# A decoder layer on one core: sums for the first block of each up projection by DMA and GpSimd, the residual turned later, the last norm by token tile

## The chip, the cores and the metric

The kernel runs on one core of one Trainium2 chip. The metric is the device time of one execution in microseconds (us). The core's engines are TensorE (PE, with its weight loads PEld), VectorE (DVE), ScalarE (ACT), GpSimd (POOL) and SyncE (SP), which issues most transfers here; each runs its own instructions in order and waits for the others by semaphores.

## The reference

One layer of a decoder: 512 tokens of 1024 features, 256 memory tokens, a feed-forward width of 2816, all fp32.

```python
def swiglu(x, w_gu, w_down):
    gate, up = jnp.split(x @ w_gu, 2, axis=-1)
    return (jax.nn.silu(gate) * up) @ w_down

def reference(x, mem, ...):
    h = x
    h = h + 0.5 * swiglu(rms_norm(h, g_ffn1), w_ffn1_gu, w_ffn1_down)
    h = h + hybrid_mixer(rms_norm(h, g_mix), ...)
    h = h + memory_cross_attention(rms_norm(h, g_cross), rms_norm(mem, g_mem), ...)
    h = h + 0.5 * swiglu(rms_norm(h, g_ffn2), w_ffn2_gu, w_ffn2_down)
    return rms_norm(h, g_final)
```

The change touches the two feed-forward parts (`swiglu`) and the last `rms_norm`.

## The kernel before

Each feed-forward part is an up projection (`up`), whose result is spilled to HBM, and a down projection (`down`). Both are computed as Strassen-Winograd products: a 2x2 split of tokens and weights takes seven products P1 to P7 instead of eight, of sums of quarters. Every fp32 operand is split in a high and a low part (`split_hi` on ScalarE, line 117; `split_lo` on VectorE, line 123), and `mm_strassen` (lines 425 to 431) makes three matmuls of each pair.

The up projection has six blocks of columns, five of 512 and a last of 256. `UP` gives the order of the products in a block: P1, P2, P5, P3, P6, P7, P4. A product has two token halves with 12 matmuls each. `BANK` says which PSUM banks they accumulate in: P3 goes on in the banks that P5 opened ("C"), P6, P7 and P4 in those of P1 ("A"). Between the two products of a bank, `evac` copies the first result out (`a_...` in the listings, line 487, by ScalarE), so P3's first matmul of a token half stands behind the copy of that half of P5.

The weights of a block come as two units (0 and 1) of 1024 columns. `Weights.load` (line 392) has SyncE load three tiles for each: `x1` (quarter b11), `x2` (b22) and `x3` (b21). `Weights.make` splits the tile that a product needs into `whi` and `wlo` and then turns it into the next sum. `EARLY`, the table for the ups, names for each product the tile to split and the tile that the sum takes: after P1 and P3 an accumulating transfer adds b12 from HBM (line 418, issued by GpSimd), after P5 VectorE adds x3 to x1 (line 420), after P6 it adds x1 to x2 (line 422). The pool has buffers for six `x1`, three `x2`, six `x3`.

The token side has four quarters a11, a21, a12, a22 in two tiles, made once per up (`prepare`). Four sums of 128x1024 (line 462, VectorE) turn them into the others: v = a22 - a21 and a21 = a11 - a21 at P5, a11 = v + a11 and a12 = a11 - a12 at P3. Each product's side is split once, in block 0, into two `s` tiles, and kept.

`Plan` emits the units four ahead of the product in turn (`UNITS_AHEAD`) and the loads five ahead of that (`LOADS_AHEAD`). A scheduler then sets the order on each engine, and a load waits until a buffer of its pool is free. In an up the products depend on the split of their weights, of their side, and on the bank.

In `down`, three sets of pairs (a, b, c: four, four and three pairs of chunks of the 2816) go through seven products in the order `DOWN` = P1, P5, P6, P3, P7, P2, P4; P1 and P5 are run as P1a, P1b, P5a, P5b, P1c, P5c. Units 4 and 5 of the weights are those of set c. The sides are read back from the spill (line 591). Each result is added to the residual in token order, `ht` (line 607). Ahead of the products stands `before`: in the first down a load of `ht`, in the second `turn_back` (line 1088), which makes `ht` by 32 transposes of `h` and eight copies on ScalarE (line 1096).

After each result's last addition `squares2` sums the squares of one half of a token tile (line 1101). At the end `both` adds the two halves' sums for all four token tiles, `ro.newton` (lines 287 to 305) makes the reciprocal roots in 12 operations on 128x4, and four operations of 128x1024 (line 1110) scale by root and gain. Four transfers of 512 KB write the output (line 1112).

## Time and profile before

| | |
|---|---|
| time, median of 3 runs | 1454.97 us (1453.27 to 1457.66) |
| profiled execution | 1453.23 us |
| its span, first to last instruction | 1451.5 us |
| mean granted TensorE clock | 0.976 |
| busy: TensorE, VectorE, ScalarE, GpSimd | 96%, 65%, 51%, 6% |
| the first up, block 0; a block without waits | 58.16 us; 39.88 us |
| the second up, block 0 | 54.83 us |
| last matmul to end | 12.97 us |

The page has the busy shares; the stretches are those of the program's blocks, from the first matmul of one to the first of the next. A matmul of 512 columns stands 0.23 us behind the one before at full clock. A wait is shown ahead of the instruction that waited, with the engine that ended it. Instructions are told by line and by their tiles with buffer numbers left out, so `x` is any weight tile and `s` any side.

### The profile page before, as it was taken

The page shows a single profiled execution, that of the slowest core. Times are in us where ns is not written, and L with a number is a line of the kernel's source. Part 1 is how long each engine was busy: PE and PEld are TensorE (multiplying, and loading weights), DVE is VectorE, ACT ScalarE, POOL GpSimd, SP SyncE. Part 2 cuts the span into 40 slices and gives each one's busy share as a digit, 9 for nine tenths or more (in the row PEclk, how much of TensorE's full clock was granted, in tenths as well). Part 3 has the DMA queues.
Part 4 walks back from the last instruction along what each step waited for, and adds up shares of the span by engine and source line. Part 5 has one row for each costly group of instructions (what it writes and reads, how often), then busy time and mean ns, then how long its engine had stood idle before and what let it go on. Part 6 is the DMA issues. An engine that isn't in the chain of part 4 may idle for free.

```text
span 1451.5 us, 16735 instructions
## 1 busy us (share of the span) xinstructions
PE 1387.9 (96%) x6548; PEld 1162.3 (80%) x6548; DVE 949.7 (65%) x1237; ACT 735.6 (51%) x947; POOL 83.3 (6%) x102
## 2 busy tenths in 40 slices
PE   8899999999899999999999999999987999987996
PEld 7688888778788888888888888988865888876885
DVE  4877777696656664676544447655448777865884
ACT  6555565464565554566332225444335555554562
POOL 0011111110000000000000000000000111101000
PEclk8999999999999999999999999999988999998998
DMA  8676666871522233222223224444165666667461
GB/s 305 145 192 183 183 181 192 270 168 54 178 83 87 65 139 106 69 87 87 88 89 114 87 90 143 145 149 142 58 203 161 181 174 166 157 203 228 123 174 58
DMA packets 48303, 207.17 MB, mean 143 GB/s; under 512 B 5152, under 2 KB 5152, under 8 KB 39392
## 3 DMA queue, kind: packets, MB, share of 16 engines
q1 hardware_dynamic: 32624, 149.22, 29.6%
q0 software_dynamic: 15600, 56.89, 17.7%
q8 instruction: 51, 0.84, 0.2%
q14 instruction: 28, 0.23, 0.0%
HBM read 183.80 MB, written 22.28 MB: 142 GB/s over the span
## 4 chain that ended last, share of the span: by engine, by line
PE 83%; issue 5%; DMA 4%; DVE 4%; ACT 3%; POOL 0%; DVEq 0%; ACTq 0%; POOLq 0%
PE ps L153 13%; PE ps L155 13%; PE ps L154 13%; PE ps L430 11%; PE ps L429 11%; PE ps L431 11%; DMA x<-in_w_gu 2%; DVE wlo L123 2%; PE ps L250 2%; PE ps L249 2%; PE ps L251 1%; PE z L809 1%; ACT whi L117 1%; DMA x<-in_w_dt 1%; PE ps L521 1%
## 5 line engine op out<-in xcount | busy, mean ns | idle before, releaser
L429 PE MATMUL ps<-whi,s 128*128 128x512 f32 (+1 forms) x980 | 379.6, 389 | 31.8 <-ACT whi L117 11.7
L430 PE MATMUL ps<-wlo,s 128*128 128x512 f32 (+1 forms) x980 | 377.1, 385 | 3.3 <-DVE wlo L123 3.2
L431 PE MATMUL ps<-whi,s 128*128 128x512 f32 (+1 forms) x980 | 376.1, 384 | 0.5 <-DVE s L123 0.5
L123 DVE TENSOR_TENSOR wlo<-x,whi 128x1024 fp32r<-128x1024 f32 (+1 forms) x238 | 281.2, 1189 | 113.5 <-ACT whi L117 112.5
L117 ACT ACTIVATE whi<-x 128x1024 fp32r<-128x1024 f32 (+1 forms) x238 | 243.8, 1031 | 214.9 <-PE ps L431 128.9
L153 PE MATMUL ps<-a,whi 128*128 128x512 f32 (+1 forms) x832 | 318.2, 383 | 3.8 <-ACT whi L117 3.8
L155 PE MATMUL ps<-a,wlo 128*128 128x512 f32 (+1 forms) x832 | 318.0, 382 | 0.0
L154 PE MATMUL ps<-a,whi 128*128 128x512 f32 (+1 forms) x832 | 317.7, 382 | 0.0
L117 ACT ACTIVATE whi<-raw 128x1024 fp32r<-128x1024 f32 x120 | 127.1, 1060 | 269.0 <-PE ps L154 177.6
L429 PEld LDWEIGHTS ps<-whi,s 128*128 128x128 f32 x980 | 188.9, 193 | 70.4 <-ACT whi L117 15.3
L430 PEld LDWEIGHTS ps<-wlo,s 128*128 128x128 f32 x980 | 188.8, 193 | 41.4 <-DVE wlo L123 7.2
L431 PEld LDWEIGHTS ps<-whi,s 128*128 128x128 f32 x980 | 188.9, 193 | 35.7 <-DVE s L123 1.0
L123 DVE TENSOR_TENSOR wlo<-raw,whi 128x1024 fp32r<-128x1024 f32 x120 | 146.5, 1222 | 84.4 <-ACT whi L117 84.2
L153 PEld LDWEIGHTS ps<-a,whi 128*128 128x128 f32 x832 | 157.1, 189 | 34.1 <-ACT whi L117 4.1
L155 PEld LDWEIGHTS ps<-a,wlo 128*128 128x128 f32 x832 | 156.9, 189 | 31.1 <-DVE wlo L123 0.8
L154 PEld LDWEIGHTS ps<-a,whi 128*128 128x128 f32 x832 | 157.0, 189 | 30.4 <-DVE a L125 0.2
L418 POOL DMA_DIRECT2D x<-in_w_gu x44 | 38.5, 874 | 1077.6 <-DVE wlo L123 1035.9
L117 ACT ACTIVATE a<-a 128x512 fp32r<-128x512 f32 (+2 forms) x61 | 34.0, 557 | 59.5 <-DVE a L113 19.3
L113 DVE TENSOR_TENSOR a<-ps,a 128x512 f32<-128x512 f32 (+1 forms) x56 | 36.1, 649 | 38.8 <-PE ps L155 38.5
L123 DVE TENSOR_TENSOR s<-s,s 128x1024 fp32r<-128x1024 f32 (+1 forms) x36 | 40.6, 1129 | 17.3 <-ACT s L117 16.3
L123 DVE TENSOR_TENSOR a<-a,a 128x512 fp32r<-128x512 f32 (+2 forms) x61 | 36.2, 600 | 15.5 <-ACT a L117 11.6
L487 ACT ACTIVATE a<-ps,ny 128x512 f32<-128x512 f32 (+1 forms) x48 | 31.0, 650 | 28.8 <-PE ps L431 27.0
(162 smaller groups left out, 1326.5 us busy)
## 6 DMA issues: line engine op xcount, KB each, us to landing
x<-in_w_gu SPq DMA_DIRECT2D x66, 512.0 KB, 6.3
x<-in_w_gu POOLq DMA_DIRECT2D x44, 512.0 KB, 5.7
spilled<-e POOLq DMA_DIRECT2D x22, 896.0 KB, 7.5
x<-in_w_dn SPq DMA_DIRECT2D x30, 512.0 KB, 5.1
s<-spilled SPq DMA_DIRECT2D x28, 512.0 KB, 4.5
x<-in_w_dn POOLq DMA_DIRECT2D x20, 512.0 KB, 7.7
raw<-in_w_qk SPq DMA_DIRECT2D x8, 1024.0 KB, 4.9
raw<-in_w_v SPq DMA_DIRECT2D x8, 1024.0 KB, 5.2
```

What stands on the lines that cost most here:

```text
L113: nc.vector.tensor_tensor(out=out_, in0=a, in1=b, op=ALU.mult)
L117: nc.scalar.activation(hi, src, AF.Copy)
L123: nc.vector.tensor_tensor(out=lo, in0=src, in1=hi.bitcast(F32), op=ALU.subtract)
L153: nc.tensor.matmul(ps, wh, xh, start=first, stop=False, **kw)
L154: nc.tensor.matmul(ps, wh, xl, start=False, stop=False, **kw)
L155: nc.tensor.matmul(ps, wl, xh, start=False, stop=last, **kw)
L249: nc.tensor.matmul(ps[t], xh[:, c], hi[:, k, :], start=kk == 0, stop=False)
L418: nc.gpsimd.dma_start(out=x, in_=self.src[u][1], accum_op=ALU.add)
L429: nc.tensor.matmul(ps, ah, bh, start=first and k == 0, stop=False, **kw)
L430: nc.tensor.matmul(ps, ah, bl, start=False, stop=False, **kw)
L431: nc.tensor.matmul(ps, al, bh, start=False, stop=last and k == len(parts) - 1, **kw)
L487: nc.scalar.activation(a[key], ps, func, scale=scale)
```

## The change

Five edits:

1. Block 0 of each up uses a third table, `DMA_ONLY`: `x1` gets all three of its sums by accumulating transfers (b12 after P1's split, b21 after P5's, b22 after P6's), and P4 splits `x1` instead of `x2`. The four additions on VectorE fall away there, and four transfers come. `x2` is free after P2's split, `x3` after P7's as before.
2. The token sums run on GpSimd, and all four are issued at P5.
3. In `down`, `before` is issued behind the first two products (P1a, P1b) instead of ahead of all.
4. The last norm runs for each token tile as soon as its two halves are final (`finish`): 13 small operations on one column, then for half 1 a product with the gain on VectorE and a scaling on ScalarE, for half 0 one operation on VectorE, and an output transfer of 256 KB for each half.
5. Units 4 and 5, which only a down has, get buffers of their own (`x1b`, `x3b`, two each), and `x1` and `x3` have four instead of six. So in an up four tiles of each can be loaded ahead, and the down's last units are loaded during the first blocks of the up.

```diff
--- before.py
+++ after.py
@@ -391,7 +391,8 @@
 
         def load(self, x, u):
             def fn():
-                t = pools["w"].tile([P, 1024], F32, tag=x, name=nm(x), bufs=xbufs[x])[:, :self.size[u]]
+                tag = x if u < 4 or x == "x2" else x + "b"
+                t = pools["w"].tile([P, 1024], F32, tag=tag, name=nm(x), bufs=xbufs[tag])[:, :self.size[u]]
                 nc.sync.dma_start(out=t, in_=self.src[u][self.STARTS[x]])
                 self.t[x, u] = t
 
@@ -399,27 +400,29 @@
 
 
 
-        EARLY = {1: ("x1", "x1"), 2: ("x2", "x2"), 5: ("x1", "x3"), 3: ("x3", "x3"), 6: ("x1", "x2"),
-                 7: ("x3", "x3"), 4: ("x2", "x2")}
-        LATE = {**EARLY, 2: ("x2", "x1"), 6: ("x1", "x1"), 4: ("x1", "x1")}
+
+        EARLY = {1: ("x1", 1), 2: ("x2", None), 5: ("x1", "x3", "x1"), 3: ("x3", 1), 6: ("x1", "x1", "x2"),
+                 7: ("x3", None), 4: ("x2", None)}
+        LATE = {**EARLY, 2: ("x2", "x2", "x1"), 6: ("x1", None), 4: ("x1", None)}
+        DMA_ONLY = {**EARLY, 5: ("x1", 2), 6: ("x1", 3), 4: ("x1", None)}
 
         def unit(self, i, u):
-            x, y = self.chain[i]
-            return self.plan.unit(lambda: self.make(i, u), max(self.at[x, u], self.at[y, u]))
+            tiles = [x for x in self.chain[i] if isinstance(x, str)]
+            return self.plan.unit(lambda: self.make(i, u), max(self.at[x, u] for x in tiles))
 
         def make(self, i, u):
-            x, y = (self.t[k, u] for k in self.chain[i])
+            x, *then = self.chain[i]
+            x = self.t[x, u]
             hi, lo = (pools["w"].tile([P, 1024], F32R, tag=tag, name=nm(tag), bufs=xbufs["w"])
                       for tag in ("whi", "wlo"))
             m = self.size[u]
             split_hi(hi[:, :m], x)
             split_lo(lo[:, :m], x, hi[:, :m])
-            if i in (1, 3):
-                nc.gpsimd.dma_start(out=x, in_=self.src[u][1], accum_op=ALU.add)
-            elif i == 5:
-                nc.vector.tensor_tensor(out=x, in0=x, in1=y, op=ALU.add)
-            elif x is not y and i in (6, 2):
-                nc.vector.tensor_tensor(out=y, in0=y, in1=x, op=ALU.add)
+            if len(then) == 2:
+                src, dst = (self.t[k, u] for k in then)
+                nc.vector.tensor_tensor(out=dst, in0=dst, in1=src, op=ALU.add)
+            elif then[0] is not None:
+                nc.gpsimd.dma_start(out=x, in_=self.src[u][then[0]], accum_op=ALU.add)
             return [(hi[:, j:j + self.n], lo[:, j:j + self.n]) for j in range(0, m, self.n)]
 
     def mm_strassen(ps, sides, units, first, last, **kw):
@@ -430,7 +433,7 @@
             nc.tensor.matmul(ps, ah, bl, start=False, stop=False, **kw)
             nc.tensor.matmul(ps, al, bh, start=False, stop=last and k == len(parts) - 1, **kw)
 
-    xbufs = dict(x1=6, x2=3, x3=6, w=5)
+    xbufs = dict(x1=4, x1b=2, x2=3, x3=4, x3b=2, w=5)
 
     def up(g, r, w_gu, begin, norm):
 
@@ -459,14 +462,13 @@
             a11, a21, a12, a22 = (box[k] for k in ("a11", "a21", "a12", "a22"))
 
             def sum_(out, a, b, op):
-                nc.vector.tensor_tensor(out=out, in0=a, in1=b, op=op)
+                nc.gpsimd.tensor_tensor(out=out, in0=a, in1=b, op=op)
 
 
             if i == 5:
                 box["v"] = half(pools["w"].tile([P, 1024], F32, tag="wlo", name=nm("v"), bufs=xbufs["w"]))
                 sum_(box["v"], a22, a21, ALU.subtract)
                 sum_(a21, a11, a21, ALU.subtract)
-            elif i == 3:
                 sum_(a11, box["v"], a11, ALU.add)
                 sum_(a12, a11, a12, ALU.subtract)
             src = {1: a11, 2: a12, 5: box.get("v"), 3: a12, 6: a11, 7: a21, 4: a22}[i]
@@ -533,7 +535,7 @@
             per = 1024 // n
             units = 4 // per
             w = Weights(plan, [[w_gu[row + q * units + u] for q in range(4)] for u in range(units)], n,
-                        Weights.EARLY)
+                        Weights.EARLY if b else Weights.DMA_ONLY)
             row += 4 * units
             for x in w.STARTS:
                 for u in range(units):
@@ -617,12 +619,13 @@
             if a + m == n:
                 evac(i, t, ps)
 
-        plan.step(before)
         cuts = list(range(0, n, 4))
 
         order = [(i, a) for i in DOWN[:2] for a in cuts[:-1]] + [(i, cuts[-1]) for i in DOWN[:2]]
         order += [(i, a) for i in DOWN[2:] for a in cuts]
-        for i, a in order:
+        for place, (i, a) in enumerate(order):
+            if place == 2:
+                plan.step(before)
             m = min(a + 4, n) - a
             sd = side(i, a, m)
             us = []
@@ -1084,7 +1087,6 @@
             gain = pools["h"].tile([P, D], F32, name="gain")
             nc.sync.dma_start(out=gain, in_=g_final.partition_broadcast(P))
             sums2 = spool.tile([P, 8], F32, name="sums2", bufs=1)
-            ro = Norm()
 
             def turn_back():
                 for t in range(4):
@@ -1096,20 +1098,33 @@
                         nc.scalar.activation(ht[:, t, half * 512:(half + 1) * 512], ps, AF.Copy)
 
             def squares2(i, t):
-                for tok, half in {2: ((t, 0),), 3: ((t, 1),), 7: ((t + 2, 1),), 4: ((t + 2, 0),)}.get(i, ()):
-                    sq = pools["a"].tile([P, 512], F32, tag="sq", name=nm("sq"))
-                    nc.scalar.activation(sq, ht[:, tok, half * 512:(half + 1) * 512], AF.Square,
-                                         accum_out=sums2[:, 4 * half + tok:4 * half + tok + 1])
+                tok, half = {2: (t, 0), 3: (t, 1), 7: (t + 2, 1), 4: (t + 2, 0)}.get(i, (None, None))
+                if tok is None:
+                    return
+                sq = pools["a"].tile([P, 512], F32, tag="sq", name=nm("sq"))
+                nc.scalar.activation(sq, ht[:, tok, half * 512:(half + 1) * 512], AF.Square,
+                                     accum_out=sums2[:, 4 * half + tok:4 * half + tok + 1])
+                if i in (2, 4):
+                    finish(tok)
+
+            def finish(tok):
+
+                ro = Norm(P)
+                both = spool.tile([P, 1], F32, tag="both", name=nm("both"))
+                nc.vector.tensor_tensor(out=both, in0=sums2[:, tok:tok + 1], in1=sums2[:, 4 + tok:5 + tok], op=ALU.add)
+                ro.newton(both)
+                for half in (1, 0):
+                    c = slice(half * 512, (half + 1) * 512)
+                    o = ht[:, tok, c]
+                    if half:
+                        mul(o, o, gain[:, c])
+                        nc.scalar.activation(o, o, AF.Copy, scale=ro.cols)
+                    else:
+                        nc.vector.scalar_tensor_tensor(out=o, in0=o, scalar=ro.cols, in1=gain[:, c], op0=ALU.mult,
+                                                       op1=ALU.mult)
+                    nc.sync.dma_start(out=out[tok][:, c], in_=o)
 
             down(spilled, ht, w_dn2, w_dt2, turn_back, squares2)
-            both = spool.tile([P, 4], F32, name="both", bufs=1)
-            nc.vector.tensor_tensor(out=both, in0=sums2[:, :4], in1=sums2[:, 4:], op=ALU.add)
-            ro.newton(both)
-            for t in range(4):
-                o = ht[:, t, :]
-                nc.vector.scalar_tensor_tensor(out=o, in0=o, scalar=ro.cols[:, t:t + 1], in1=gain, op0=ALU.mult,
-                                               op1=ALU.mult)
-                nc.sync.dma_start(out=out[t], in_=o)
 
 
 def _tiles(w):
```

Three places show how the instructions now stand. First GpSimd's queue at the start of the second up: `x_8282` and `x_8284` are the `x1` tiles of units 0 and 1, `x_8290` and `x_8292` the `x3` tiles, `x_8268` holds a11 and a21, `x_8269` a12 and a22; `x_8299` and later are of block 1. Before:

```order
L418 DMA x_8282<-in_w_gu 128x1024
L418 DMA x_8284<-in_w_gu 128x1024
L418 DMA x_8290<-in_w_gu 128x1024
L418 DMA x_8292<-in_w_gu 128x1024
L418 DMA x_8299<-in_w_gu 128x1024
L418 DMA x_8311<-in_w_gu 128x1024
```

Now:

```order
L425 DMA x_8282<-in_w_gu 128x1024
L425 DMA x_8284<-in_w_gu 128x1024
L465 TENSOR_TENSOR v_8323<-x_8269,x_8268 128x1024
L465 TENSOR_TENSOR x_8268<-x_8268 128x4x256
L465 TENSOR_TENSOR x_8268<-v_8323,x_8268 128x4x256
L425 DMA x_8282<-in_w_gu 128x1024
L465 TENSOR_TENSOR x_8269<-x_8268,x_8269 128x4x256
L425 DMA x_8284<-in_w_gu 128x1024
L425 DMA x_8290<-in_w_gu 128x1024
L425 DMA x_8292<-in_w_gu 128x1024
L425 DMA x_8282<-in_w_gu 128x1024
L425 DMA x_8284<-in_w_gu 128x1024
```

The four sums stand behind P1's two transfers, and the second transfer into each `x1` stands among or behind them; a third into each follows those of `x3`.

Second, ScalarE in the same block: `whi_8454` and `whi_8459` are the splits of P6's weights, `a_8437` and `a_8452` the copies of P5's two token halves, `s_8376`, now `s_8372`, is P3's side. Before:

```order
L117 ACTIVATE whi_8410<-x_8290 128x1024
L117 ACTIVATE whi_8415<-x_8292 128x1024
L117 ACTIVATE whi_8454<-x_8282 128x1024
L487 ACTIVATE a_8437<-ps_8424,negr_8267 128x512
L117 ACTIVATE s_8376<-x_8269 128x1024
L499 ACT_TABLE_LOAD
L499 ACTIVATE a_8343<-a_8343 128x512
L499 ACTIVATE a_8358<-a_8358 128x512
L119 ACTIVATE s_8420<-x_8268 128x1024
L487 ACTIVATE a_8452<-ps_8439,negr_8267 128x512
L117 ACTIVATE whi_8459<-x_8284 128x1024
```

Now:

```order
L117 ACTIVATE whi_8408<-x_8290 128x1024
L117 ACTIVATE s_8372<-x_8269 128x1024
L117 ACTIVATE whi_8415<-x_8292 128x1024
L501 ACT_TABLE_LOAD
L501 ACTIVATE a_8345<-a_8345 128x512
L119 ACTIVATE s_8420<-x_8268 128x1024
L501 ACTIVATE a_8360<-a_8360 128x512
L489 ACTIVATE a_8437<-ps_8424,negr_8267 128x512
L117 ACTIVATE whi_8454<-x_8282 128x1024
L117 ACTIVATE whi_8459<-x_8284 128x1024
L489 ACTIVATE a_8452<-ps_8439,negr_8267 128x512
```

Both splits for P6 stand between P5's two copies; P6's first stood ahead of the first copy and the second behind the last one before.

Third, ScalarE where the second down begins: `e` are the last columns' turned results, which are spilled then, `ht` the copies of the turned residual; `whi_10273` (now `whi_10225`) is the first split for P5a. Before:

```order
L117 ACTIVATE whi_10273<-x_10191 128x1024
L523 ACTIVATE e_10112<-ps_10113 128x512
L523 ACTIVATE e_10112<-ps_10119 128x512
L1096 ACTIVATE ht_10137<-ps_10141 128x512
L1096 ACTIVATE ht_10137<-ps_10147 128x512
```

Now:

```order
L117 ACTIVATE whi_10225<-x_10143 128x1024
L525 ACTIVATE e_10112<-ps_10113 128x512
L525 ACTIVATE e_10112<-ps_10119 128x512
L117 ACTIVATE whi_10232<-x_10145 128x1024
L117 ACTIVATE whi_10317<-x_10149 128x1024
L117 ACTIVATE whi_10324<-x_10151 128x1024
L117 ACTIVATE s_10239<-s_10177 128x1024
L1098 ACTIVATE ht_10137<-ps_10267 128x512
```

Three more splits of weights and one of a side now stand ahead of the first `ht` copy.

## Rows read from the trace of the kernel before

**Rows 1.** The page, its span and the busy time of each engine.

```profile
span 1451.5 us, 16735 instructions
...
PE 1387.9 (96%) x6548; PEld 1162.3 (80%) x6548; DVE 949.7 (65%) x1237; ACT 735.6 (51%) x947; POOL 83.3 (6%) x102
```

**Rows 2.** Stretch, us; busy PE, PEld, DVE, ACT, POOL; PEclk, DMA share, GB/s.

```profile
32.12:68.62 36.50, 30.98 (x121) 24.37 (x120) 30.71 (x33) 20.02 (x23) 3.44 (x4) 0.91 0.57 140
81.21:108.50 27.29, 27.29 (x123) 22.61 (x122) 19.03 (x23) 14.81 (x18) 4.21 (x5) 1.00 0.94 251
256.31:292.23 35.92, 31.49 (x140) 24.90 (x138) 22.78 (x25) 16.92 (x21) 3.87 (x5) 1.00 0.84 260
1088.64:1129.46 40.82, 32.94 (x121) 25.39 (x121) 32.79 (x33) 23.20 (x27) 3.44 (x4) 0.87 0.58 157
1091.65:1101.75 10.10, 8.98 (x24) 6.36 (x25) 10.10 (x10) 7.32 (x9) 0.00 (x0) 0.66 0.07 30
1318.47:1363.57 45.10, 37.12 (x174) 30.92 (x173) 25.73 (x28) 21.68 (x29) 3.38 (x4) 0.89 0.65 184
1438.53:1451.50 12.97, 0.00 (x0) 0.00 (x0) 7.69 (x18) 0.72 (x2) 0.00 (x0) 0.64 0.40 162
```

**Rows 3.** Timeline of TensorE, second up: start, us, instructions [idle before <- releaser].

```profile
1088.03 0.39 PE L430 MATMUL ps<-wlo,s 128*128 128x512 f32 x1
1088.26 0.39 PE L431 MATMUL ps<-whi,s 128*128 128x512 f32 x1
1091.65 0.50 PE L429 MATMUL ps<-whi,s 128*128 128x512 f32 x1 [3.01 <-ACT s L117]
...
1116.85 0.73 PE L429 MATMUL ps<-whi,s 128*128 128x512 f32 x2 [3.73 <-ACT whi L117]
```

**Rows 4.** Timeline of TensorE, block 0 of the first up.

```profile
39.84 0.73 PE L429 MATMUL ps<-whi,s 128*128 128x512 f32 x2 [2.11 <-ACT s L117]
...
43.25 0.80 PE L429 MATMUL ps<-whi,s 128*128 128x512 f32 x1 [2.21 <-ACT s L119]
```

**Rows 5.** Chain of waits, start of the second up: start, us, what.

```profile
1076.40 0.85 POOL x L418
...
1077.28 12.22 DMA x<-in_w_gu
```

**Rows 6.** DMA issues: how many, KB each, median us to landing.

```profile
x<-in_w_gu POOLq DMA_DIRECT2D x44, 512.0 KB, 5.7
...
out_t<-ht SPq DMA_DIRECT2D x4, 512.0 KB, 2.8
```

**Rows 7.** Timeline of SyncE, start of the second up.

```profile
1066.21 11.74 SPq L395 DMA_DIRECT2D x<-in_w_gu  x15
```

**Rows 8.** Line 462, the token sums: durations min/median/max, first and last start.

```profile
L462 DVE TENSOR_TENSOR v<-x,x x2: 1217/1217/1217, 26.5 to 1080.3; 128x1024 f32<-128x1024 f32 x2
```

**Rows 9.** Timeline of GpSimd, start of the first up.

```profile
12.17 1.99 POOL L418 DMA_DIRECT2D x<-in_w_gu  x2 [10.66 <-DVE wlo L123]
```

**Rows 10.** Groups of GpSimd's own work: busy, mean ns, idle before.

```profile
L707 POOL MEMSET fence<- 128x512 f32 x1 | 0.5, 526 | 52.1 <-ACT sq L682 52.1
L710 POOL TENSOR_SCALAR_AFFINE_SELECT fence<-fence 128x256 f32<-128x256 f32 x1 | 0.4, 393 | 0.0
...
L103 POOL MEMSET ones<- 128x128 f32 x1 | 0.2, 204 | 0.3 <-POOLq L1209 0.3
```

**Rows 11.** Timeline of TensorE, start of the second down.

```profile
1319.99 3.11 PE L1094 MATMUL ps<-ident,h 128*128 128x128 f32 x27
1331.08 0.80 PE L429 MATMUL ps<-whi,s 128*128 128x512 f32 x1 [7.98 <-ACT ht L1096]
```

**Rows 12.** Chain of waits, start of the second down.

```profile
1324.39 5.88 DMA spilled<-e
```

**Rows 13.** Timeline of VectorE, the tail.

```profile
1440.11 0.16 DVE L1106 TENSOR_TENSOR both<-sums 128x4 f32<-128x4 f32 x1 [0.85 <-ACT sq L1101]
...
1442.68 4.87 DVE L1110 SCALAR_TENSOR_TENSOR ht<-ht,ny,gain 128x1024 f32<-128x1024 f32 x4
```

## The prediction, made before the change was run

> **What bounds the kernel now.** I read the page first. TensorE is busy 96% of a span of 1451.5 us [rows 1], so only its idle time, its time at the lower clock and the tail can be won; the other engines matter through what TensorE waits for. The profiled execution took 1453.23 us, 1.74 under the median of the runs; the sums are made against it.
>
> Next the busy time by stretch [rows 2]. From P5 on, the last five products of an undisturbed block take 27.29 us. The same five take 36.50 in block 0 of the first up and 40.82 in the second, where TensorE is busy 30.98 and 32.94 at a granted clock of 0.91 and 0.87. So at most 9.2 and 13.5 us can be won there. In the second down, the time from the last up product to the start of P6 is 45.10, in the first 35.92. After the last matmul 12.97 us pass.
>
> Then TensorE's timeline in those stretches, for what ended each wait. Second up: P2's last matmul begins at 1088.26 and they stand 0.23 apart; P5 then waits 3.01 us for `s` on ScalarE and P7 3.73 for a `whi` [rows 3]. First up: P3 waits 2.11 and, for its second token half, 2.21, both for `s` [rows 4]. A wait costs more than itself: P5 of the second up, which follows one, takes 10.10 at clock 0.66 [rows 2] (between its two levels, 1.2 and 2.4 GHz, so about two thirds of it at half clock) against 5.44, 24 matmuls at 0.227. The chain of waits names the origin [rows 5]: the accumulating transfer of P5's second weight sum, issued 1077.28, lands 12.22 later, while the median of its kind is 5.7 [rows 6]; 15 loads were issued from 1066.21 on, most of them ahead of it [rows 7].
>
> **Weight sums and buffers.** Per up, four VectorE additions of 128x1024 (1.22 us each, as the token sums of that shape [rows 8]) go and four accumulating transfers come, issued in 0.87 us each on POOL (two in 0.85 and more at 1076.40, two in 1.99 at 12.17 [rows 5, 9]). VectorE is rid of 4.9 us, which TensorE does not see by itself. What counts is when the sums land. With four x1 and x3 buffers 9 loads are free at the start of an up instead of 15; the tenth waits for the split of P2's first tile. So the first sums, for P5, meet a shorter burst. I take a landing 5.7 to 9 us after issue: in the second up the last comes between 1083.0 and 1086.3, before P2 ends, and P5 starts near 1088.6 without its 3.01.
>
> The second sums, for P6, can leave only when P5's weights are split: about 1088 and 1089 to 1091 for the two units. They land 5.7 to 12.22 later; the later unit between 1094.7 and 1101.4, both taken with an early issue for the late landing. **This is the new wait.** On ScalarE the splits of these sums (`whi_8454`, `whi_8459`) now stand ahead of `a_8452`, the copy of P5's second token half, and P3 accumulates into the bank that this copy empties. Without a wait P3's second half would start at 1088.6 + 5.44 + 2.72 = 1096.8. The copy, about 1.7 us behind the landing, ends between 1096.4 and 1103.1: a stall of 0 to 6.3, and up to 4.7 more for slow matmuls behind it (10.10 less 5.44). From 13.5 that leaves 2.5 to 13.4; **I take 9**, as the sums leave when few loads are under way. In the first up the same order holds (`whi_364`, `whi_369`, `a_362`): the two waits of [rows 4] go, the second sums leave about 28 and land between 34 and 41, against 40.3 for P3's second half, with a side split and three copies behind them on ScalarE. Off the 9.2 goes a stall of 1.2 to 5.2, with up to 4.7 behind it: -0.7 to 8, **I take 4**.
>
> **Token sums on GpSimd.** Eight of 128x1024, four per up. No row shows an addition on POOL. Nearest are fills of 128x512 (526 ns) and 128x128 (204), so 0.84 ns a column and 0.1 us fixed, and a select of 128x256 in 393 [rows 10]: one pass over 1024 columns is 1.0 us, three (two operands and a result) 2.8; these are the ends. I take two passes, 1.9, since the select, which reads and writes, is over a fill's rate (0.32 by that). In the second up POOL has issued both first sums at 1077.28 + 0.87 = 1078.2; v ends at 1080.1, the third sum at 1083.9, and only the fourth stands behind an issue that waits for P5's split, done at about 1091. P3's side needs it at 1094.1. Even at 2.8 the first three end at 1086.6, before that split. Nothing is on the path: cost 0, with up to 1 of the range for ends at 2.8.
> The Trainium skill, page GPSIMD Engine Reference, section Performance versus the Vector engine, speaks against this move: it gives an fp32 addition of 2048 columns as 4497 ns on GpSimd and 2293 on VectorE. An estimate from that page is 2.25 us for 1024 columns; no run here shows it yet, and by it the sum would be the same.
>
> **Residual turned later.** 32 transposes of 128x128 (27 of them in 3.11 [rows 11], so 3.7 in all) and eight copies leave the place behind the last up product and now stand behind two products of the down, whose spilled tiles landed long ago. So P1's first two products run while the last spill lands (5.88 us from 1324.39 [rows 12]), where TensorE now waits 7.98 [rows 11]. The first down, where the residual comes by a transfer, is the model: 35.92 [rows 2], plus 3.7 is 39.6 against 45.10, a gain of 5.5. Of those 35.92, 4.43 are idle (31.49 busy at full clock), for weight sums of the down's last pieces; with the new buffers these pieces are loaded in block 0 or 1, so up to 9.9. **I take 9**, nearer the end without waits. If P5 must wait for copies and banks, the 3.7 count twice at most, 5.5 again.
>
> **Last norm per token tile.** Before, 13 small operations of about 0.2 run from 1440.11, then four scaled products in 4.87 from 1442.68 [rows 13], and an output of 512 KB takes 2.8 [rows 6]. Now three token tiles are done before the last half product ends. Left are the 13 (2.6 us), a multiplication and a scaled product of 128x512, 0.61 each (an eighth of 4.87), and 256 KB to write: 1440.11 + 2.6 + 1.2 = 1443.9, or 1445.4 with some of another tile's work ahead, against 1447.55. Gain 1.5 to 3.5, **2**. The 39 small operations more on VectorE lie beside P2 and P4, where no wait was.
>
> The first down, the last blocks and the middle I leave at 0: their loads start earlier, nothing else. Sum: 4 + 9 + 9 + 2 = 24, 1453.23 - 24 = 1429.2; with part of the 1.74 to the median, **1430**.
>
> **The rivals.**
> 1. The second sums land late, so both blocks give nothing and 9 + 2 remain: 1442 on the profiled execution's own scale, 1443 with the median's part at most, I say 1441. For: the 12.22 in the chain, and four more accumulating transfers per up. Against: they leave after the burst. Chance 0.20.
> 2. All fits and no stall follows: 8 + 13.4 + 9 + 2 = 32.4, about 1421. For: GpSimd is busy 6% [rows 1] and VectorE is eased. Against: the order on ScalarE. Chance 0.20.
> 3. Slower: GpSimd's sums become the bound, four in a row on one in-order queue that also issues the weight sums. With T for one sum, P3's side in the second up is ready at 1078.2 + 4T + 0.9 + 2.3 (an issue, a split on two engines) against 1101.75 today, in the first at 14.2 + 4T + 3.2 (POOL free at 12.17 + 1.99 [rows 9]) against 39.84. At T = 6.5 this is 5.6 and 3.6 late, the second weight sums behind them lose about 2 more, and the 11 of the down and the tail are gone: there it decides. At T = 7.5 it loses 9.6 + 7.6, so 1453.2 - 11 + 17 = 1459. For: no row shows an operation on POOL with two operands, nor one beside a busy VectorE. Against: every row of POOL's own work is under 0.6 us [rows 10], T would be over twice my upper end. Chance 0.03.
> The Trainium skill, page SBUF — State Buffer, section SBUF: two separate sides, has a rule that would feed this: a VectorE operation with two SBUF inputs and a GpSimd operation lock a shared pair of ports against each other, for the whole instruction. No run here shows it yet.
> 4. It moves little: waits of equal length take the place of those removed, the down's among them, 1454. Chance 0.05.
>
> **How the numbers follow.** The forecast has 0.52. The range runs from just under rival 2 to just over rival 1, 1419 to 1443; the ends of the terms fall into it unless all come together. About 0.3%, 4.4 us, is what a measurement of this kernel can tell from no change. The forecast and rivals 1 and 2 are beyond that, 0.92; I give 0.90, since a rival 1 that loses at the down too would be within it: same 0.06, slower 0.04.
>
> **What would show it.** Right: P5 of the second up starts at the end of P2; in block 0 one wait is left, before P3's second half, for an `a` copy; no 7.98 at the second down, whose P5 begins about 9 us earlier against the last up product; the tail 2 us shorter; sums of 1.0 to 2.8 us on GpSimd. Wrong: waits for accumulating transfers before P6; sums over 3 us on POOL, with VectorE's operations longer beside them; P5 of the down waiting for `ht` copies.

## The result and the profile after

The changed kernel took 1440.62 us (median of 4 runs, 1434.07 to 1442.71) against 1454.12 for the kernel before: a ratio of 0.9896, 95% interval 0.9864 to 0.9928. That is faster by 13.5 us where 24 were forecast, and inside the range; the interval of the ratio lies below 1, though the gain is under 2%. The profiled execution is the fastest of the four, 1434.07 us; against the profile of before it gains 19.2.

The page of the changed kernel, its span and busy times (before: [rows 1]):

```profile
span 1432.1 us, 16800 instructions
...
PE 1384.2 (97%) x6548; PEld 1160.5 (81%) x6548; DVE 949.7 (66%) x1264; ACT 737.9 (52%) x951; POOL 112.0 (8%) x118
```

GpSimd has 29 us more. The stretches of the changed kernel (before: [rows 2]), in time's order: from P5 of the first up to its block 1, the first down to P6, block 0 of the second up whole and from P5 on, the second down to P6, the tail (columns as there):

```profile
31.56:64.31 32.75, 29.38 (x122) 23.50 (x120) 24.52 (x30) 20.55 (x24) 5.50 (x7) 0.95 0.98 242
252.46:291.56 39.10, 33.89 (x140) 27.19 (x139) 23.29 (x26) 17.40 (x21) 3.87 (x5) 0.91 0.79 240
1073.71:1122.40 48.69, 44.28 (x168) 33.95 (x169) 42.40 (x33) 29.34 (x33) 19.96 (x14) 0.91 0.98 264
1088.07:1122.40 34.33, 30.22 (x121) 23.26 (x120) 28.04 (x27) 20.44 (x23) 9.31 (x9) 0.95 0.95 234
1311.81:1346.39 34.58, 34.58 (x174) 28.92 (x173) 23.24 (x25) 21.14 (x29) 3.39 (x4) 1.00 0.82 237
1422.48:1432.10 9.62, 0.00 (x1) 0.00 (x0) 5.16 (x27) 2.17 (x4) 0.00 (x0) 0.76 0.29 109
```

Against before there are 3.75 and 6.1 us less in the two blocks (the second took 54.83 before), 10.5 less at the second down and 3.35 less in the tail. The first down is **3.2 longer**, and from P6 on the second down lost 1.1. Block 0 of the second up shows two engines in each other's way. GpSimd's timeline, then VectorE's:

```profile
1075.45 1.76 POOL L425 DMA_DIRECT2D x<-in_w_gu  x2 [705.40 <-DVE wlo L123]
1076.91 2.69 POOL L465 TENSOR_TENSOR v<-x,x 128x1024 f32<-128x1024 f32 x1
1079.67 3.27 POOL L465 TENSOR_TENSOR x<-x 128x1024 f32<-128x1024 f32 x1
1083.03 3.26 POOL L465 TENSOR_TENSOR x<-v,x 128x1024 f32<-128x1024 f32 x1
...
1088.87 2.65 POOL L465 TENSOR_TENSOR x<-x,x 128x1024 f32<-128x1024 f32 x1
```

```profile
1077.10 10.27 DVE L123 TENSOR_TENSOR wlo<-x,whi 128x1024 fp32r<-128x1024 f32 x3
...
1088.43 5.31 DVE L123 TENSOR_TENSOR wlo<-x,whi 128x1024 fp32r<-128x1024 f32 x2
```

Three splits took 10.27 us while three sums ran, and two took 5.31 beside the fourth; pairs of them away from the sums took 2.36 in this profile. TensorE's timeline, second up and then first up:

```profile
1092.66 0.57 PE L433 MATMUL ps<-wlo,s 128*128 128x512 f32 x1 [2.68 <-DVE wlo L123]
...
1098.63 0.50 PE L432 MATMUL ps<-whi,s 128*128 128x512 f32 x1 [0.22 <-ACT a L489]
```

```profile
40.83 0.50 PE L432 MATMUL ps<-whi,s 128*128 128x512 f32 x1 [3.30 <-ACT a L489]
```

The 3.01 ahead of P5 in the second up is gone; a wait of 2.68 for a weight split stands inside P5. In the first up P3 waits 3.30 for the copy of P5's result; on ScalarE it stands behind a split for P6 that waited for its sum:

```profile
37.04 1.06 ACT L117 ACTIVATE whi<-x 128x1024 fp32r<-128x1024 f32 x1 [4.64 <-DMA x<-in_w_gu]
38.00 1.04 ACT L119 ACTIVATE s<-x 128x1024 fp32r<-128x1024 f32 x1
38.95 1.25 ACT L489 ACTIVATE a<-ps,ny 128x512 f32<-128x512 f32 x2
40.09 0.68 ACT L489 ACTIVATE a<-ps,negr 128x512 f32<-128x512 f32 x1
```

At the second down the transposes stand in one row, with no wait ahead of them or of the down [rows 11]:

```profile
1323.60 3.65 PE L1096 MATMUL ps<-ident,h 128*128 128x128 f32 x32
```

At the first down TensorE waits for a split, whose sum hangs in the chain of waits for 15.28 us. First TensorE's row, then GpSimd's timeline, then the chain:

```profile
283.48 0.49 PE L432 MATMUL ps<-whi,s 128*128 128x512 f32 x1 [4.45 <-ACT whi L117]
```

```profile
263.78 0.79 POOL L677 DMA_DIRECT2D ht<-in_xr  x1 [4.75 <-DMA spilled<-e]
266.99 0.91 POOL L425 DMA_DIRECT2D x<-in_w_dn  x1 [2.42 <-DVE wlo L123]
```

```profile
266.99 15.28 DMA x<-in_w_dn
```

The 2 MB load of the residual was issued 3.2 us ahead of that sum, on the same queue.

SyncE's loads at the start of the second up have changed too. Before, 15 were issued within 11.74 us [rows 7]. Now nine go out, and the tenth waits 9.0 us for a split on VectorE, that of P2's first tile. First SyncE's timeline up to 1078, then its wait behind it:

```profile
1065.27 4.28 SPq L396 DMA_DIRECT2D x<-in_w_gu  x9
```

```profile
SPq L396 <- DVE wlo L123: 9.0, 1, 9.0
```

The held loads follow in one go, eight of them from 1080.71 to 1085.91. In the first up eight held loads leave from 25.01 to 28.29, around the first of the second weight sums (27.70):

```profile
25.01 1.76 SPq L396 DMA_DIRECT2D x<-in_w_gu  x4
...
28.29 0.46 SPq L396 DMA_DIRECT2D x<-in_w_dt  x1
```

### The profile page after: what moved, and what is told of

The parts are those of the page before. It is cut to its first block, busy times and chain, and to the rows that moved or that the text cites. A ratio compares the mean times of both kernels' runs of the same rounds, so it can differ in the third digit from the quotient of the medians.

```text
span 1432.1 us, 16800 instructions
## 1 busy us (share of the span) xinstructions
PE 1384.2 (97%) x6548; PEld 1160.5 (81%) x6548; DVE 949.7 (66%) x1264; ACT 737.9 (52%) x951; POOL 112.0 (8%) x118
## 3 DMA queue, kind: packets, MB, share of 16 engines
q0 software_dynamic: 16752, 61.09, 19.4%
## 4 chain that ended last, share of the span: by engine, by line
PE 79%; issue 7%; DMA 5%; DVE 5%; ACT 3%; POOL 1%; ACTq 0%; POOLq 0%; DVEq 0%
PE ps L153 13%; PE ps L155 13%; PE ps L154 13%; PE ps L433 10%; PE ps L434 10%; PE ps L432 10%; DMA x<-in_w_gu 3%; DVE wlo L123 2%; DMA x<-in_w_dn 2%; PE ps L250 2%; PE ps L249 2%; PE ps L251 2%; PE z L812 1%; ACT whi L117 1%; PE ps L523 1%
## 5 line engine op out<-in xcount | busy, mean ns | idle before, releaser
L123 DVE TENSOR_TENSOR wlo<-x,whi 128x1024 fp32r<-128x1024 f32 (+1 forms) x238 | 291.6, 1232 | 114.3 <-ACT whi L117 113.1
L425 POOL DMA_DIRECT2D x<-in_w_gu x52 | 45.6, 876 | 1037.8 <-DVE wlo L123 1030.6
L423 DVE TENSOR_TENSOR x<-x,x 128x1024 f32<-128x1024 f32 (+1 forms) x60 | 71.0, 1188 | 1.2
```

Source lines behind the costliest of these rows:

```text
L123: nc.vector.tensor_tensor(out=lo, in0=src, in1=hi.bitcast(F32), op=ALU.subtract)
L423: nc.vector.tensor_tensor(out=dst, in0=dst, in1=src, op=ALU.add)
L425: nc.gpsimd.dma_start(out=x, in_=self.src[u][then[0]], accum_op=ALU.add)
```

## The experiments

Every version is the changed kernel with the edits named. Each expectation was put down before its run; it has a theory and a rival to it. The table has each profile's stretches in us: A, first up from P5 to block 1; B, block 0 of the second up; C, first down to P6; D, second down to P6; T, tail. The times are medians, with the ratio to the kernel before on the same chip; versions ran on different chips, so times are compared by ratio.

| version | A | B | C | D | T | time, ratio (95%) |
|---|---|---|---|---|---|---|
| before | 36.50 | 54.83 | 35.92 | 45.10 | 12.97 | 1 |
| changed | 32.75 | 48.69 | 39.10 | 34.58 | 9.62 | 1440.62, 0.9896 (0.9864 to 0.9928) |
| changed, again | 32.95 | 49.40 | 38.32 | 37.31 | 9.62 | 1436.70, 0.9865 (0.9836 to 0.9894) |
| sums on VectorE | 37.01 | 51.41 | 35.50 | 35.70 | 9.56 | 1444.90, 0.9922 (0.9895 to 0.9949) |
| residual turned first | 31.53 | 48.89 | 38.83 | 45.43 | 9.58 | 1445.93, 0.9934 (0.9911 to 0.9958) |
| old norm | 32.47 | 49.01 | 38.57 | 34.56 | 12.94 | 1440.73, 0.9895 (0.9871 to 0.9920) |
| old table of weight sums | 28.96 | 48.64 | 38.74 | 34.59 | 9.63 | 1433.15, 0.9835 (0.9811 to 0.9860) |
| P6's splits held | 32.92 | 51.35 | 39.18 | 37.07 | 9.58 | 1439.46, 0.9880 (0.9854 to 0.9906) |
| held, sums on VectorE | 34.56 | 48.37 | 37.17 | 34.37 | 9.65 | 1434.14, 0.9837 (0.9807 to 0.9867) |
| residual loaded in steps | 32.69 | 50.01 | 33.09 | 34.37 | 9.64 | 1433.48, 0.9841 (0.9812 to 0.9870) |
| old table, sums on VectorE | 36.30 | 52.54 | 35.26 | 34.69 | 9.65 | 1441.81, 0.9924 (0.9903 to 0.9945) |
| six buffers | 33.71 | 49.00 | 36.96 | 35.48 | 9.61 | 1435.23, 0.9889 (0.9857 to 0.9921) |
| old table, residual in steps | 28.98 | 48.53 | 33.97 | 34.37 | 9.62 | 1432.20, 0.9860 (0.9835 to 0.9885) |
| the same, fourth sum on VectorE | 32.49 | 47.72 | 33.39 | 36.27 | 9.68 | 1431.00, 0.9853 (0.9827 to 0.9879) |

**The changed kernel again**, unaltered.

> The changed kernel once more, unaltered: its runs spread from 1434.07 to 1442.71 us while its profile shows the fastest, 1434.07. Theory: the spread sits in one stretch that hangs on the landing of a transfer (the first down, where P1c waits 4.45 us for a weight sum that took 15.28 to land), so a profile of a slower execution shows that stretch longer by 4 to 8 us and all others equal within 1. Rival: the spread is in all stretches alike (each some tenths longer), as a different chip or clock would give.

Its four executions took 1435.09 to 1442.0; the profile is of the slowest. It is 8.0 us longer than the first profile, and neither theory holds: C is 0.8 shorter, but the start of the first up (P1 to P5) is 23.80 instead of 20.89, the last block of the second up 31.95 instead of 29.86, D 2.7 longer. These three places wander over all versions (20.8 to 24.7, 28.3 to 32.7, and D, where the residual is turned late, 34.4 to 37.3), so two versions are compared by stretch first.

**Token sums on VectorE.**

```diff
-                nc.gpsimd.tensor_tensor(out=out, in0=a, in1=b, op=op)
+                nc.vector.tensor_tensor(out=out, in0=a, in1=b, op=op)
```

> The changed kernel with the four token sums of each up back on VectorE, still all at P5. Theory: a GpSimd sum and a two-operand VectorE operation exclude each other (in the second up three weight splits take 10.27 us beside the sums instead of 3.5), so with the sums on VectorE the wait of 2.68 for wlo in P5 of the second up goes, its block 0 gets 3 to 5 us shorter and that of the first up 0 to 3; 3 to 6 us in all. Rival: VectorE is the loaded engine at that place, its four sums of 1.22 put the same 4.9 us ahead of the splits, and the time is the same within 2 us or longer.

The theory falls: A and B are 4.3 and 2.7 longer. TensorE's row in the first up:

```profile
48.04 1.65 PE L432 MATMUL ps<-whi,s 128*128 128x512 f32 x3 [6.62 <-ACT s L119]
```

It waits for a side on ScalarE. The scheduler's order there had changed with the sums: in both ups P6's first split, which waits for its transfer, now stood ahead of P3's side (in the second up `whi_8454` ahead of `s_8372`).

**Residual turned first**: `before` at place 0 instead of 2.

> The changed kernel with the load or turning of the residual ahead of the down's products again. Theory: it costs about 10 us at the second down (7.98 of waiting behind the last spill and the low clock after it come back) and nothing, 0 to 2, at the first. Rival: the new place moves the wait to P6 or to the last products of the down, and it costs only some 5; or at the first down the old place is better by 3, as the first down of the changed kernel is 3.2 longer, so it costs 6 to 7.

D goes back to 45.43 and C stays, which is the theory; TensorE's row at the second down shows the old wait. From P6 on the down took 74.97 instead of 76.09; versions with the later place take 75.25 to 76.12 there, so it gives back 0.3 to 1.1.

```profile
1328.72 0.80 PE L432 MATMUL ps<-whi,s 128*128 128x512 f32 x1 [8.37 <-ACT ht L1098]
```

**The old norm**, over four token tiles at the end.

> The changed kernel with the last norm over all four token tiles at the end again. Theory: the tail after the last matmul goes from 9.6 back to about 13.0 us and the time rises by 3.3. Rival: the per-tile work slows VectorE in the second down's P4 (P6 of the second down shows a new idle of 0.8), so 1 of it is given back, and the time rises by 2 or less.

The tail goes back to 12.94, 3.3 longer, as the theory had it; the time is 4.0 above the changed kernel on the same chip, whose own executions spread over 7, so the time alone would not show it. P6 to the last matmul stays at 76.06: the new norm did not cause the 1.1.

**The old table of weight sums in block 0**, token sums still on GpSimd.

```diff
-                        Weights.EARLY if b else Weights.DMA_ONLY)
+                        Weights.EARLY)
```

> The changed kernel with the old table of weight sums in block 0 (four additions on VectorE, four accumulating transfers less), the token sums still on GpSimd. Theory: in block 0 VectorE is what TensorE waits for (wlo in P5), so four additions of 1.22 us put back there make the five products from P5 on 2 to 5 us longer in each up, 4 to 8 in all. Rival: the additions lie in gaps of VectorE and save transfers that land late, so the five products take the same within 1 us in each up and the time is unchanged.

Both theories expected no gain, and there is one: A falls by 3.8, B stays, the time is the lowest of the one-part versions. The windows of A and of the second up from P5 on:

```profile
34.33:63.29 28.96, 27.77 (x122) 22.37 (x120) 26.36 (x29) 19.37 (x23) 3.48 (x4) 1.00 0.68 168
...
1088.03:1122.29 34.26, 30.98 (x121) 24.33 (x120) 31.42 (x31) 23.11 (x26) 5.00 (x5) 0.90 0.67 173
```

VectorE has more to do and TensorE less to wait. Four accumulating transfers issued from 27.70 to 34.90 took 9.2, 9.5, 10.4 and 12.5 us in the changed kernel; here the first up has two, from 38.19, that took 5.6 and 5.8. So **the new table of weight sums costs time in the first up and gives none in the second**.

It need not be the number of accumulating transfers that costs. In the changed kernel's second up four leave from 1088.25 to 1096.97, about as close together, and take only 5.7 to 7.8 us. In the first up they leave among the eight held loads, the last of which lands at 47.19. With the old table SyncE does not stop after nine loads: all 15 are issued by 20.09 and landed by 33.28, ahead of these two transfers. The late landings go with these loads; no run parts them from the transfers themselves.

**P6's splits held** behind the copy of P5's second half on ScalarE; then the same **with the sums on VectorE**.

```diff
-            split_hi(hi[:, :m], x)
+            if i == 6 and self.chain is self.DMA_ONLY:
+                with tc.issue_after(self.copied):
+                    split_hi(hi[:, :m], x)
+            else:
+                split_hi(hi[:, :m], x)
...
+                    w.copied = copy(("u", t2), ps, minus[t2]).ins
```

> The changed kernel with P6's two weight splits of block 0 issued on ScalarE behind the copy of P5's second half. Theory: the order of the record (a copy behind splits that wait for transfers) was not what held P3 up, since P3 of the second up waited only 0.22 us; the five products from P5 on stay within 1 us (32.9 and 34.3 to 35.0). Rival, the prediction's step: that order is the remaining wait of block 0, and the five products get 2 to 4 us shorter in each up.

The time is the same, which goes against the rival, and A stays at 32.92 as the theory has it; B is 2 to 2.7 longer, which neither has. The wait moved: P3 of the first up waits 0.47 instead of 3.30, and TensorE waits ahead of P7, in the first up and in the second:

```profile
52.43 0.63 PE L436 MATMUL ps<-whi,s 128*128 128x512 f32 x1 [2.83 <-DVE a L496]
```

```profile
1113.78 0.47 PE L436 MATMUL ps<-whi,s 128*128 128x512 f32 x1 [2.57 <-DVE a L496]
```

In the first up the chain of waits behind the 2.83 goes through splits and a copy to the landing of a weight sum, P7's:

```profile
35.32 12.36 DMA x<-in_w_gu
```

The order did hold P3 up, yet when it is mended the late sums hold up the next products instead.

> As the run before, but with the token sums on VectorE. With the sums on VectorE and the scheduler's own order, a split of P6's weights stood ahead of P3's side on ScalarE, and the five products took 37.0 and 36.9 us instead of 32.8 and 34.3. Theory: that order is the whole loss, and GpSimd's sums gain nothing by themselves (they hold VectorE's splits up while they run); with the order held the five products come down to 31 to 34 in both ups, level with the run before or 1 to 3 us shorter. Rival: VectorE's extra 4.9 us are the loss; they stay at 36 to 37.

With the order held, VectorE's version comes from 37.01 to 34.56 in A and from 51.41 to 48.37 in B: level with GpSimd's in B (48.69 to 49.40), 1.7 behind in A. The theory holds nearly, the rival does not: most of GpSimd's lead with this table is the order that the scheduler chose for it. With the order held, the time is even lower with the sums on VectorE, 1434.14 against 1439.46 on one chip, though the intervals of the two ratios just overlap.

**The first down's residual in two steps.**

```diff
-            nc.gpsimd.dma_start(out=ht, in_=xr.rearrange("t p d -> p t d"))
+            nc.gpsimd.dma_start(out=ht[:, :2, :512], in_=xt_[:, :2, :512])
...
+                with tc.issue_after(w.acc):
+                    nc.gpsimd.dma_start(out=ht[:, 2:, :], in_=xt_[:, 2:, :])
+                    nc.gpsimd.dma_start(out=ht[:, :2, 512:], in_=xt_[:, :2, 512:])
```

> The changed kernel with the first down's residual loaded in two steps: 512 KB that P1 needs at the old place, 1.5 MB behind the weight sums of the last pieces on GpSimd's queue. Theory: the 2 MB load ahead of those two sums on that queue is what makes them land 15 us after issue and TensorE wait 4.45 + 0.76; with 512 KB ahead the first down from P1a to P6 goes from 38.3 to 39.1 to 32.5 to 35, and the time falls by 4 to 6. Rival: the seven side loads from the spill crowd the engines as much; the sums land 2 us earlier at most and the stretch stays over 36.

The theory holds: C falls by 6.0 to 33.09 (31.50 busy, full clock), and the sum lands 9.8 us after issue. In the stretch from P6 to P4 1.3 is given back (61.17 for 59.83).

```profile
253.23:286.32 33.09, 31.50 (x139) 24.89 (x138) 22.69 (x25) 16.80 (x21) 5.34 (x7) 1.00 0.93 283
```

**Old table and sums on VectorE**, buffers, residual and norm as changed (sums at P5 and P3 as before).

> The changed kernel with its first two edits undone: block 0 has the old table of weight sums, and the token sums are on VectorE, two at P5 and two at P3. The buffers, the later residual and the last norm stay. With the old table and GpSimd's sums the five products from P5 on took 29.0 and 34.3 us. Theory: GpSimd's sums are worth it with either table; here the five products take 33 to 36.5 and 36 to 38 again, and the time is 5 to 10 above that run. Rival: the buffers alone, which shorten the burst of loads, made block 0 faster; then they stay within 1.5 of 29.0 and 34.3 and the time with them.

The theory holds: A 36.30 and B 52.54 against 28.96 and 48.64 with GpSimd's sums, and a ratio of 0.9924 against 0.9835. The first sums of the second up took 9.5 and 12.1 us to land, as before. With the new buffers, 15 loads are still issued from 1071.15 to 1082.56, as before; the rival, the buffers, is out. B is 2.3 below the 54.83 of before; this was not looked into.

**Six buffers.**

```diff
-    xbufs = dict(x1=4, x1b=2, x2=3, x3=4, x3b=2, w=5)
+    xbufs = dict(x1=6, x2=3, x3=6, w=5)
```

(with one tag for all units)

> The changed kernel with six buffers for x1 and x3 as before and none of their own for the down's last pieces. Theory: 15 loads instead of 9 go out ahead of the first sums, the second of these lands about 12 instead of 8.5 us after issue in the second up, P5 waits some 3 us there, and the time rises by 2 to 5. Rival: the landing does not hang on how many loads stand ahead, or P5 waits for wlo anyway; the same within 1.5.

A and B stay within 1, and the first sums of the second up land 7.1 and 9.0 us after issue (changed: 6.8 and 8.5). The new buffers move nothing that these profiles can tell. But this is no evidence for the rival, that the landing does not hang on the loads ahead, because the condition of the theory did not come about: with six buffers nine loads go out as well, and the tenth waits 9.0 us for the same split.

```profile
1066.69 6.36 SPq L396 DMA_DIRECT2D x<-in_w_gu  x9
```

So **the number of loads ahead goes with the table, not with these buffers**: nine with `DMA_ONLY`, with four buffers or six; 15 with the old table, with four buffers or six. With `DMA_ONLY` block 0's `x2` is free after P2's split, and the next `x2` load, the tenth, waits for one of that tile's three buffers at the head of SyncE's queue. The landings go with it: in the fourteen profiles 5.8 to 7.1 and 7.8 to 9.5 us behind nine loads, 9.1 to 9.6 and 11.9 to 12.2 where 15 go out.

**The old table with the residual in two steps**, the version that the runs point to.

> The changed kernel with the old table of weight sums in block 0 (sums on GpSimd kept) and the first down's residual loaded in two steps. Theory: the two gains lie in different stretches and add up; the five products at 29 and 34.3, the first down to P6 at 33, a time of 1426 to 1430, 9 to 12 under the changed kernel. Rival: the late part of the residual delays something else of the first down (its P6 to P4 stretch was 1.1 longer), and the sum is 1431 to 1433.

By stretch the gains add up: A 28.98, C 33.97. The median is where the rival put it, 1431 to 1433. The profiled execution took 1427.01, the other three 1432.18 to 1433.35, all four below the fastest of the changed kernel's. The ratio's interval overlaps that of the changed kernel; the two were not run on one chip.

**The same with the fourth sum on VectorE**, since here TensorE waits for the split of P5's side in the second up. VectorE's, GpSimd's and TensorE's rows of the version above:

```profile
1081.64 3.40 DVE L123 TENSOR_TENSOR s<-v,s 128x1024 fp32r<-128x1024 f32 x1
```

```profile
1080.70 3.26 POOL L465 TENSOR_TENSOR x<-x,x 128x1024 f32<-128x1024 f32 x1
```

```profile
1085.10 0.50 PE L434 MATMUL ps<-whi,s 128*128 128x512 f32 x1 [2.07 <-DVE s L123]
```

> The fastest version so far (old table in block 0, residual of the first down in two steps) with the fourth token sum of each up on VectorE, the other three on GpSimd. Theory: the two engines exclude each other; in the second up the split of P5's side takes 3.40 us instead of 1.2 beside GpSimd's fourth sum, and TensorE waits 2.07 for it and runs slower behind. With that sum gone from GpSimd the wait goes, and the stretch from P5 to the next block falls from 34.1 to 30.5 to 32.5; a time 1 to 3 us lower. Rival: the sum's 1.2 us now stand in VectorE's own queue behind GpSimd's third sum and ahead of P5's second weight split, the wait is the same or longer, and nothing is won.

With that sum gone from GpSimd, the split and TensorE's waits in the second and the first up are:

```profile
1084.32 1.21 DVE L123 TENSOR_TENSOR s<-v,s 128x1024 fp32r<-128x1024 f32 x1
```

```profile
1089.00 0.50 PE L433 MATMUL ps<-wlo,s 128*128 128x512 f32 x1 [1.80 <-DVE wlo L123]
...
51.56 1.26 PE L432 MATMUL ps<-whi,s 128*128 128x512 f32 x3 [3.37 <-ACT whi L117]
```

The exclusion is shown, 3.40 against 1.21 for the same split; its price is not won back. The wait became one of 1.80 for the next split (from P5 on 33.32 instead of 34.14), and in the first up the wait ahead of P7 grew from 1.20 to 3.37 (A 32.49 instead of 28.98). The time is the same, as the rival has it.

## Why the prediction was right and where it was not

Term by term, the forecast first, then the two profiles of the changed kernel:

- **First up, 4: 3.75 and 3.55.** Size and mechanism held: ScalarE's copy of P5 stands behind P6's split (`a_347` behind `whi_364`), and P3 waits 3.30, at its first half already. The term lumped two effects of opposite sign: with the old table, moving the sums to GpSimd and issuing all four at P5 is worth 7.3 (36.30 to 28.96; engine and place were not parted there), and the new table takes back 3.8.
- **Second up, 9: 6.1 and 5.4** (whole block). P5 does start at P2's end. The reason given was a shorter burst, nine loads because of four buffers. The burst is nine loads and the sums land in the forecast time, but the cause is the table and not the buffers, and P5 does not need it: with the old table the sums land as late as before (11.9 us for the second) and P5 starts at P2's end all the same, since with GpSimd's sums the scheduler puts P5's side ahead of the second weight split (`s_8328` ahead of `whi_8367` in the changed kernel). So that P5 came out on time is in part luck. And "nothing is on the path: cost 0" for the sums on GpSimd failed: they shut VectorE's splits out, which stands as the 2.68 in P5 (with the sums on VectorE, P5 waits 0.61, 0.53 and 0.85). It was noted under the slower rival, with no term of its own. The wait forecast, of P3's second half, did not come; P3 waits 0.22 at its first.
- **GpSimd's sums, 1.0 to 2.8 each with 1.9 taken:** 2.37 to 3.27, longest beside VectorE. The prediction's own sign of being wrong, sums over 3 us beside longer operations of VectorE, came. The Trainium skill, page GPSIMD Engine Reference, section Performance versus the Vector engine, gave 2.25 by estimate; the first v, 2.39 in the first up, is 6% above it. Its comparison, a ratio of 1.96 for VectorE, would leave the sums there; in the scheduler's own order the runs go the other way, the kernel is faster with them on GpSimd under either table (A and B together: 81.4 to 82.4 against 88.4, 77.6 against 88.8); with the order held it is not.
- **Second down, 9: 10.5 and 7.8**, and turning it back costs 10.8. P1 runs during the spill as forecast; up to 1.1 came back from P6 on, which was not seen.
- **Tail, 2: 3.35**, near the upper end of the 1.5 to 3.5 that were given.
- **First down, 0: 3.2 and 2.4 longer.** This is the step that failed most: "their loads start earlier, nothing else". The weight sums that the down's last pieces need landed 15.28 us after issue instead of 12.59. That the residual's load ahead of them costs time is shown by its split, which takes 6.0 off; but that load stood there before too, so why the change made it 3.2 worse is open. One thing goes with it: in the changed kernel the second side load is issued 0.14 us ahead of the residual's load, before 0.14 behind. With one side load ahead (four profiles with the whole load, before among them) that load lands after 11.9 to 13.2 us and C is 35.3 to 37.2; with two (seven) it is 13.7 to 15.4 and 37.0 to 39.2. The two groups meet, and the four are also the versions with the token sums on VectorE, so these profiles don't part the two.

The terms of the first profile sum to 3.75 + 6.1 + 10.5 + 3.35 less 3.2 and 1.1, 19.4, against the 19.2 between the profiled executions. The median gains only 13.5, as this execution was the fastest: in the others some places are 2 to 4 us longer each. Why they wander was not settled. Rival 1 had the time (1441) but not the reason: the second sums do land late in the first up, yet both blocks gained.

## What to carry to other kernels

When a sum moves to another engine, ask what the scheduler does with everything behind it: with the new table the order on ScalarE, an engine that the change did not touch, decided more than the sums' own time. Ask also which buffer a change frees and which load then stands first in its queue: here nine loads left instead of 15, and the held ones met the next transfers. A transfer that replaces an operation of 1.2 us on an engine with gaps can lose: accumulating transfers took 9 to 12 us among these loads and 5.6 to 5.8 without. And a large load that is not needed yet does not belong on a queue ahead of a small transfer that is: 512 KB in place of 2 MB took 6 us off.

## What the hardware showed that was not expected

An operation of VectorE with two operands in SBUF and one of GpSimd exclude each other: 1.21 us for a split alone, 3.40 beside a sum, 10.27 for three beside three sums. The Trainium skill, page SBUF — State Buffer, section SBUF: two separate sides, says that they lock a shared pair of ports for a whole instruction; these rows agree. GpSimd's sums stretch too, 2.37 to 3.26 for the same addition, a11, in the first and in the second up.
